# Shift and scale columns ahead of the first loop's blocks, and two gates computed early and parked in DRAM

## The chip, the cores and the metric

The kernel runs on one core of a Trainium2 chip. The metric is the device time of one execution in microseconds, the median of several runs. TensorE (PE in the rows) does matmuls and their weight loads (PEld), VectorE is DVE, ScalarE is ACT, GpSimd is POOL and SyncE is SP. Each engine runs its own instructions in the order of the program and waits where an input or a buffer isn't ready.

## The reference, cut to what matters

One block of a diffusion model on x (512 tokens of 1024 columns) with a context of 256 tokens:

```python
mx = split(silu(c) @ w_mod + b_mod, 6)         # shift, scale, gate, shift, scale, gate of x
mc = split(silu(c_ctx) @ w_mod + b_mod, 6)     # the context uses shift and scale only
hx = rms_norm(x, g_mix) * (1 + mx[1]) + mx[0]
hc = rms_norm(ctx, g_mix) * (1 + mc[1]) + mc[0]
conv, qa, kva, kr, gates = split(hx @ w_in)    # the context: hc @ w_in for kva and kr alone
y_conv = silu(layer_norm(depthwise(a * sigmoid(g)))) @ w_pw          # a, g = split(conv)
y_mla = attention(qa, kva, kr, kva_c, kr_c) @ w_o                    # 8 heads
x = x + mx[2] * ((sigmoid(g_conv) * y_conv + sigmoid(g_mla) * y_mla) @ w_out)   # split(gates)
x = x + mx[5] * swiglu(modulate(rms_norm(x), mx[3], mx[4]));  out = rms_norm(x)
```

## The kernel before

Everything lies transposed: 128 columns of the model on the partitions, tokens along the row, so x is eight tiles of 128x512. A float32 product is made of three matmuls: each operand is split into a high part (a cast on ScalarE, `wh`, `ph`) and a low part (the difference, on VectorE, `wl`, `pl`), and high by high, high by low and low by high are added. A projection of 128 columns, `gemm`, is thus 24 matmuls of 128x512. Weights come as tiles of 512 KB (`wr`), each split in two halves of 512 columns; six halves of high and of low parts are held at a time.

**Ahead of the loop** the squares of x are added up, column sums over the partitions (`colsum`, fp32, each matmul two records) give the rms, GpSimd takes the power, and a 128x512 matmul broadcasts it (`spread`). `warm` issues matmuls of ones that nothing reads.

**The first loop** goes over the eight 128-row blocks k of x. Block k needs its shift and scale, two 128-entry columns that are dot products of silu(c) with 1024 rows of w_mod. Before, a block's slabs (1 MB) are multiplied and added on VectorE (`gemv`, six of eight 128x256 slabs) and finished on TensorE (`mod_sum`: the two others and the sum over partitions, 12 records). Then t = x * rms * (1 + scale), hh is its high part plus shift on ScalarE and hl the low part on VectorE, and 18 matmuls add the block to six accumulators (the query and key-value latents and the rotary key). ScalarE scales the same slabs by silu(c_ctx) and GpSimd adds them up for the context (`ctx_steps`, `ctx_sum`).

**The section behind it** normalises the latents, computes the first two convolution inputs (`conv_steps`: two gemms of 24 matmuls, a tanh, a multiply-add and a split; `pump` issues so many of its steps between other work), the context's modulated hc, the context's key-value latent (`pkv`, 48 matmuls of 128x256 from two weights `wk`), and then the first query projection (`prep_qr`). `rc = bcast(dg_c, C)` broadcasts the context's rms from the diagonal `dg_c`. From the first load to the first head's values the order of all engines is the order of the code; behind that, a scheduler sets it when the program is built.

**The tail** of the attention computes sixteen gates (`gate`: a gemm and a tanh): eight for the attention, eight for the convolution. `tot` adds up the eight convolution outputs and `mean` is a matmul of ones with it.

The lines that the rows name: L126 and L122 are the low and high part of a weight, L262 the multiply-add of `gemv`, L272 `mod_sum`, L278 `warm`, L184 `spread`, L189 `colsum`, L583 t, L600, L604 and L606 the loop's matmuls, L318 the matmuls of a stepped gemm, L643 the latents' multiply-add, L728 and L734 the context's, L795 the additions of `tot`, L212 the multiply-adds of the later modulation vectors.

Of the kernel before, what the change touches and what calls it, by code (L numbers as in the profile page):

```python
# [62 lines left out]
def block_kernel(ctx: ExitStack, tc: tile.TileContext, I, out):  # L63
# [186 lines left out]
    def slab(k, kc):  # L250
        return mods[k][kc // 2][:, (kc % 2) * 256:(kc % 2) * 256 + 256]

    gm, sss = [], {}

    def gemv(k, a, b):
        if a == 0:
            gm.append(bp.tile([P, 512], F32, tag="ph", name=nm("gm"), bufs=3)[:, 0:256] if PE_KC[k] < 8 else None)
        for kc in range(a, min(b, 8 - PE_KC[k])):
            if kc == 0:
                dve.tensor_scalar(out=gm[k], in0=slab(k, kc), scalar1=sc[:, kc:kc + 1], scalar2=None, op0=ALU.mult)  # L260
            else:
                dve.scalar_tensor_tensor(out=gm[k], in0=slab(k, kc), scalar=sc[:, kc:kc + 1],  # L262
                                         in1=gm[k], op0=ALU.mult, op1=ALU.add)

    def mod_sum(k, m=None, n=0):
# [1 line left out]
        for j in range(2):
            ops = [(slab(k, kc), sc[:, kc:kc + 1]) for kc in range(8 - n, 8)]
            if m is not None:
                ops.append((m, ones[:, 0:1]))  # L270
            for i, (l, r) in enumerate(ops):
                pe.matmul(ps[:, j:j + 1], lhsT=l[:, j * P:(j + 1) * P], rhs=r, start=i == 0, stop=i == len(ops) - 1)  # L272
        return ps
# [17 lines left out]

    def ctx_steps():
        for k in range(KD):
            for kc in range(KD):
                act.activation(slab(k, kc), slab(k, kc), AF.Copy, scale=sc[:, 8 + kc:9 + kc])
                if kc == KD - 1:
                    ctx_sum(k)
                yield

    def ctx_sum(k):  # L300
        md = mods[k]
# [889 lines left out]
```

## Time and profile before

| | |
|---|---|
| median of 3 runs | 1043.89 us (1043.16 to 1043.91) |
| the profiled execution | 1043.18 us, span 1041.4 us |
| TensorE busy | 1007.6 us, 97% of the span |
| VectorE, ScalarE, GpSimd busy | 582.9, 459.1, 213.2 us |
| granted clock of TensorE, mean | 0.988 |
| read from HBM | 108.65 MB, 106 GB/s over the span |

The span is the time from the first to the last instruction of the profiled execution; its own time is 1.8 us longer. A granted clock of 1.00 is 2.4 GHz, 0.50 is 1.2 GHz. Where a row of the timeline ends with brackets, the engine was idle for so long before it, and the name is that of what ended the wait.

### The profile page before, as it was taken

How to read it: one execution, taken by the hardware profiler on the slowest of the kernel's cores; microseconds unless marked ns; L12 is line 12 of the kernel's file. 1: busy time of each engine (PE TensorE's matmuls, PEld its weight loads, DVE VectorE, ACT ScalarE, POOL GpSimd, SP SyncE). 2: the span in 40 equal slices, each digit the busy share in tenths (PEclk: the TensorE clock that was granted, in tenths of full speed). 3: DMA queues.
4: the chain of work that ended last, by engine and by line, in shares of the span. 5: the costliest groups of instructions: out<-in, count | busy, mean ns of one | idle time of the engine just before them, and what ended most of it. 6: DMA issues, size and time to landing. Idle time of an engine off the chain costs nothing.

```text
span 1041.4 us, 14089 instructions
## 1 busy us (share of the span) xinstructions
PE 1007.6 (97%) x5156; PEld 851.9 (82%) x5156; DVE 582.9 (56%) x1006; ACT 459.1 (44%) x864; POOL 213.2 (20%) x343
## 2 busy tenths in 40 slices
PE   8789999999999999999999999999999999999996
PEld 7567788888888888788878888988888888888886
DVE  6997774655654554436797774744643333433332
ACT  4567465555555555634382233442333333322322
POOL 2767503252352435420000000300000000000000
PEclk9889999999999999999999999999999999999998
DMA  9901543554554626752637754132633223233312
GB/s 329 332 13 48 125 141 95 134 137 114 161 127 110 155 53 161 202 148 87 213 118 249 225 169 140 61 112 101 212 101 100 82 102 100 89 86 106 92 56 81
DMA packets 52117, 137.11 MB, mean 132 GB/s; under 512 B 8784, under 2 KB 10960, under 8 KB 52048
## 3 DMA queue, kind: packets, MB, share of 16 engines
q1 hardware_dynamic: 41808, 110.77, 33.0%
q0 software_dynamic: 10240, 25.44, 10.4%
q8 instruction: 40, 0.66, 0.3%
q14 instruction: 29, 0.24, 0.1%
HBM read 108.65 MB, written 2.10 MB: 106 GB/s over the span
## 4 chain that ended last, share of the span: by engine, by line
PE 82%; DVE 7%; DMA 3%; issue 3%; ACT 2%; POOL 2%; SPq 0%; POOLq 0%; DVEq 0%; ACTq 0%
PE px L138 13%; PE px L139 13%; PE px L140 13%; PE ps L139 9%; PE ps L138 9%; PE ps L140 9%; PE px L318 6%; PE ps L475 3%; DVE gm L262 2%; PE ps L476 2%; PE px L495 2%; DMA ur<-u 1%; DMA p<-in_w_q_dram 1%; PE px L439 1%; POOL ur L338 1%
## 5 line engine op out<-in xcount | busy, mean ns | idle before, releaser
L126 DVE TENSOR_TENSOR wl<-wr,wh 128x512 fp32r<-128x512 f32 (+2 forms) x280 | 189.5, 683 | 251.9 <-ACT wh L122 245.0
L122 ACT CAST wh<-wr 128x512 fp32r<-128x512 f32 (+1 forms) x290 | 174.5, 610 | 317.8 <-PE ps L139 138.0
L139 PE MATMUL px<-a,wh 128*128 128x512 f32 (+1 forms) x607 | 223.9, 369 | 2.7 <-DVE a L734 2.1
L138 PE MATMUL px<-a,wh 128*128 128x512 f32 (+1 forms) x607 | 224.5, 371 | 0.9 <-ACT a L105 0.6
L140 PE MATMUL px<-a,wl 128*128 128x512 f32 (+1 forms) x607 | 223.4, 368 | 0.0
L139 PE MATMUL ps<-a,wh 128*128 128x512 f32 (+1 forms) x376 | 141.5, 376 | 0.8 <-DVE a L933 0.8
L138 PE MATMUL ps<-a,wh 128*128 128x512 f32 (+1 forms) x376 | 141.5, 376 | 0.0
L140 PE MATMUL ps<-a,wl 128*128 128x512 f32 (+1 forms) x376 | 141.2, 375 | 0.0
L139 PEld LDWEIGHTS px<-a,wh 128*128 128x128 f32 x607 | 114.9, 189 | 23.2 <-DVE a L734 2.5
L138 PEld LDWEIGHTS px<-a,wh 128*128 128x128 f32 x607 | 114.9, 189 | 21.4 <-ACT a L105 1.4
L140 PEld LDWEIGHTS px<-a,wl 128*128 128x128 f32 x607 | 115.1, 190 | 18.7
L174 POOL TENSOR_TENSOR s<-s,mhalf 128x2 f32<-128x2 f32 (+1 forms) x10 | 9.4, 937 | 585.2 <-DVE s L172 585.2
L338 POOL DMA_DIRECT2D ur<-u x128 | 67.9, 538 | 114.0 <-issue 58.2
L139 PEld LDWEIGHTS ps<-a,wh 128*128 128x128 f32 x376 | 70.7, 188 | 14.1 <-DVE a L933 1.5
L138 PEld LDWEIGHTS ps<-a,wh 128*128 128x128 f32 x376 | 70.8, 188 | 12.9
L140 PEld LDWEIGHTS ps<-a,wl 128*128 128x128 f32 x376 | 70.7, 188 | 12.8
L352 POOL DMA_DIRECT2D a<-e x128 | 63.1, 499 | 86.6 <-ACT e L350 69.5
L318 PE MATMUL px<-a,wh 128*128 128x512 f32 x256 | 80.7, 393 | 0.0
L475 PE MATMUL ps<-a,a 128*128 128x512 f32 x160 | 58.1, 399 | 0.0
L318 PEld LDWEIGHTS px<-a,wh 128*128 128x128 f32 x256 | 47.1, 188 | 9.5
L212 DVE SCALAR_TENSOR_TENSOR a<-p,sc,a 128x512 f32<-128x512 f32 x56 | 40.7, 747 | 20.9 <-DMA p<-in_w_mod_dram 20.5
L318 PE MATMUL px<-a,wl 128*128 128x512 f32 x128 | 50.2, 392 | 0.0
(202 smaller groups left out, 1550.3 us busy)
## 6 DMA issues: line engine op xcount, KB each, us to landing
wr<-in_w_dram SPq DMA_DIRECT2D x60, 512.0 KB, 3.4
wr<-in_w_in_dram SPq DMA_DIRECT2D x35, 512.0 KB, 3.7
ur<-u POOLq DMA_DIRECT2D x128, 130.0 KB, 4.3
p<-in_w_mod_dram SPq DMA_DIRECT2D x64, 256.0 KB, 4.2
a<-in_w_mod_dram SPq DMA_DIRECT2D x32, 256.0 KB, 5.7
a<-e POOLq DMA_DIRECT2D x128, 64.0 KB, 2.0
wr<-in_w_dwx_dram SPq DMA_DIRECT2D x8, 512.0 KB, 3.6
wr<-in_w_o_dram SPq DMA_DIRECT2D x8, 512.0 KB, 4.9
```

What stands on the lines that cost most here:

```text
L122: act.copy(h, raw[:, i * WB:i * WB + h.shape[-1]])
L126: (eng or dve).tensor_tensor(out=l, in0=raw[:, i * WB:i * WB + h.shape[-1]], in1=h.bitcast(F32), op=ALU.subtract)
L138: pe.matmul(ps, lhsT=wh, rhs=ah, start=first, stop=False)
L139: pe.matmul(ps, lhsT=wh, rhs=al, start=False, stop=False)
L140: pe.matmul(ps, lhsT=wl, rhs=ah, start=False, stop=last)
L212: dve.scalar_tensor_tensor(out=acc[e], in0=md, scalar=sc[:, kc:kc + 1], in1=acc[e], op0=ALU.mult, op1=ALU.add)
L262: dve.scalar_tensor_tensor(out=gm[k], in0=slab(k, kc), scalar=sc[:, kc:kc + 1], in1=gm[k], op0=ALU.mult, op1=ALU.add)
L318: pe.matmul(ps, lhsT=l, rhs=r, start=k == 0 and i == 0, stop=k == n - 1 and i == 2)
L338: pool.dma_start(out=ur[32 * s_:32 * s_ + 32].bitcast(F32), in_=u[32 * g:32 * g + 32, :, 8 * s_:8 * s_ + UW].bitcast(F32))
L352: pool.dma_start(out=parts[j][32 * g:32 * g + 32, :], in_=e[32 * j:32 * j + 32, j:j + S])
L475: pe.matmul(s[:, 0:512], lhsT=l[:, q0:q0 + P], rhs=rx_, start=i == 0, stop=i == 4)
L476: pe.matmul(s[:, 512:768], lhsT=l[:, q0:q0 + P], rhs=rc_, start=i == 0, stop=i == 4)
```

## The change

The shift columns of a block come from eight fp32 matmuls with two columns on the right (`shift_dots`, for c and c_ctx together), two blocks ahead. The scale column of a block comes from one VectorE instruction of 128x1024 (`scale_dot`, which multiplies transposed weights with a row `crow` of silu(c) on all partitions and accumulates along the row), one block ahead. `gemv`, `mod_sum`, `ctx_steps` and `ctx_sum` go, and with them GpSimd's additions; all low parts of the loop are VectorE's. The context's scale takes eight more such dots (`ctx_dots`) behind the loop, from the same weights loaded again. The nine warming matmuls stand right ahead of the loop, the last three go.

In the section behind, all of conv 0 is issued first, the column sums of the context's squares are 16 matmuls instead of GpSimd additions and two, conv 1 is issued whole ahead of hc, and the first two convolution gates are computed between the context's steps and written to DRAM. In the tail these two gates are loaded back.

```diff
-PE_KC = (2, 2, 2, 2, 2, 2, 2, 2)
+EARLY = 2
...
     def load_mod(k):
-        t = [slot() for _ in range(4)]
-        for j in range(4):
-            sp.dma_start(out=t[j], in_=I["w_mod01"][k, :, 2 * j:2 * j + 2, :])
-        mods.append(t)
+        t = [slot() for _ in range(2)]
+        for j in range(2):
+            sp.dma_start(out=t[j], in_=I["w_mod0"][k, :, 512 * j:512 * j + 512])
+        mods.append((t, load_md(k)))
...
+    def row_dot(md, row, col):
+        dve.scalar_tensor_tensor(out=md, in0=md, scalar=1.0, in1=row, op0=ALU.mult, op1=ALU.mult, accum_out=col)
...
+    def shift_dots(k):
         ps = tiny(2)
...
+        for kc in range(8):
+            pe.matmul(ps, lhsT=mods[k][0][kc // 4][:, (kc % 4) * P:(kc % 4 + 1) * P], rhs=sc[:, 2 * kc:2 * kc + 2],
+                      start=kc == 0, stop=kc == 7)
+        act.copy(mod_s[:, 2 * k:2 * k + 2], ps)
+
+    def scale_dot(k):
+        row_dot(mods[k][1], crow, mod_s[:, 16 + k:17 + k])
...
+    def gate_steps(i):
+        ps = ps_x()
+        yield from mm_steps(ps, gate_ws[i], hx)
+        t = slot()
+        act.activation(t, ps, AF.Tanh, scale=0.5)
+        pool.dma_start(out=spill[i], in_=t)
...
-        warm(WARM[1])
+        r = rstd_cols(st, D, 4)
+        scale_dot(0)
+        shift_dots(0)
         w = w_slots(768)
         w_hi(w, wq[0])
-        gemv(0, 0, GA)
-        r = rstd_cols(st, D, 4)
-        w_lo(w, wq[0], pool)
-        gemv(0, GA, 8)
-        ps = mod_sum(0, gm[0], PE_KC[0])
+        ss = shift_scale(0)
         bc = spread(r, 4, tiny)
-        warm(WARM[2])
+        shift_dots(1)
+        warm(WARM[1])
...
+            if nxt:
+                scale_dot(k + 1)
+            dve.scalar_tensor_tensor(out=hl, in0=t, scalar=ss[:, 0:1], in1=hh.bitcast(F32), op0=ALU.add, op1=ALU.subtract)
+            for j in range(6):
+                pe.matmul(accx[j], lhsT=wc(w[0], j * P), rhs=hh, start=k == 0, stop=False)
             if nxt:
                 w2 = w_slots(768)
                 w_hi(w2, wq[k + 1])
...
+                ss = shift_scale(k + 1)
+                w_lo(w2, wq[k + 1])
+            if k + 2 < KD:
+                shift_dots(k + 2)
...
+        def ctx_dots():
+            for k in range(KD):
+                row_dot(mds[k], ccrow, mod_s[:, 24 + k:25 + k])
+                if k + 4 < KD:
+                    mds.append(load_md(k + 4))
+                yield
...
+        pump(steps, 12)
+        bc_q = bcast(dg_q, S)
+        latent_lo(latent_t(accx[2:4], "g_kv", bc_kv, kva, S), kva)
         rope_sum(accx[4], tk, 0)
...
+        cw += [split_w(load_c[2])]
+        for i, sq in enumerate(cq):
+            colsum(st_c, sq, 2, i == 0, i == KD - 1)
+        pump(steps, 99)
+        raw8 += [load_w(I["w_in"][19 + i]) for i in range(EARLY)]
+        tq = latent_t([accx[0], accx[1], q2], "g_q", bc_q, qa, S)
+        r_c = rstd_cols(st_c, D, 2)
+        cw += [split_w(load_c[3])]
+        latent_lo(tq, qa)
+        dg_c = diag(r_c, C)
+        pump(dots, 4)
+        gate_ws[0] = split_w(raw8[0])
...
+        pump(dots, 99)
+        steps = conv_steps(1, cw[2], cw[3])
+        u1 = next(steps)
+        pump(steps, 12)
         rc = bcast(dg_c, C)
         pump(steps, 99)
...
+            if k == 0:
+                gate_ws[1] = split_w(raw8[1])
             if k in WK_AT:
-                wk.append(split_w(load_w8[len(wk)], D, pool if LO_P[1 + len(wk)] else dve))
-        pump(steps, CONV1)
+                pump(gates, 24)
+                wk.append(split_w(load_w8[len(wk)]))
+        pump(gates, 99)
...
-        sg_conv = [gate(19 + i, o_t[6]) for i in range(2)]
+        sg_conv = []
+        for i in range(EARLY):
+            t = slot()
+            act.copy(t[:, 0:1], o_t[6][:, 0:1])
+            sp.dma_start(out=t, in_=spill[i])
+            sg_conv.append(t)
```

On VectorE, in the first loop, one block before (`gm` is the running sum of the slabs `a`, `s` the block's shift and scale, `p` the weight):

```order
L260 TENSOR_SCALAR gm_575<-a_341,sc 128x256
L262 SCALAR_TENSOR_TENSOR gm_575<-a_341,sc,gm_575 128x256
L262 SCALAR_TENSOR_TENSOR gm_575<-a_342,sc,gm_575 128x256
L282 TENSOR_SCALAR s_579<-px_541,vec 128x1
L283 TENSOR_SCALAR s_579<-px_541,bm_86,vec 128x1
L583 SCALAR_TENSOR_TENSOR t_582<-a_120,s_579,a_276 128x512
L262 SCALAR_TENSOR_TENSOR gm_575<-a_342,sc,gm_575 128x256
L262 SCALAR_TENSOR_TENSOR gm_575<-a_343,sc,gm_575 128x256
L591 SCALAR_TENSOR_TENSOR a_99<-t_582,s_579,a_98 128x512
L262 SCALAR_TENSOR_TENSOR gm_575<-a_343,sc,gm_575 128x256
L126 TENSOR_TENSOR wl_587<-p_349,wh_585 128x512
L126 TENSOR_TENSOR wl_588<-p_349,wh_586 128x256
```

The same block's worth after (`md` is the transposed weight, `row` is crow):

```order
L563 SCALAR_TENSOR_TENSOR t_455<-a_123,s_413,a_280 128x512
L257 SCALAR_TENSOR_TENSOR md_285,mod_s<-md_285,row_133 128x1024
L570 SCALAR_TENSOR_TENSOR a_101<-t_455,s_413,a_100 128x512
L279 TENSOR_SCALAR s_472<-mod_s,bm_90,vec 128x1
L120 TENSOR_TENSOR wl_468<-p_287,wh_466 128x512
L120 TENSOR_TENSOR wl_469<-p_287,wh_467 128x256
```

Six instructions on `gm` and two small ones become one long dot and one small one, and the order between t, the low part of the activation (L591, now L570) and the weight's low parts stays.

On VectorE, in the section, before, from the variance of the context (L172) to hc (L626 is the diagonal dg_c, L650 the low parts of the query latent, L332 and L106 the end of conv 0):

```order
L172 TENSOR_SCALAR s_1002<-px_822 128x2
L712 TENSOR_TENSOR s_1006<-px_822,vec 128x8
L713 TENSOR_TENSOR s_1006<-px_822,bm_86 128x8
L714 TENSOR_TENSOR s_1006<-s_1006,vec 128x8
L626 TENSOR_TENSOR a_1010<-cst,s_1004 128x256
L650 TENSOR_TENSOR a_812<-a_989,a_811 128x512
L650 TENSOR_TENSOR a_814<-a_992,a_813 128x512
L650 TENSOR_TENSOR a_816<-a_995,a_815 128x512
L332 SCALAR_TENSOR_TENSOR t_954<-t_954,px_956 128x512
L106 TENSOR_TENSOR u_823<-t_954,u_823 128x512
L728 SCALAR_TENSOR_TENSOR t_1070<-a_351,s_1006,a_1035 128x256
L728 SCALAR_TENSOR_TENSOR t_1074<-a_351,s_1006,a_1035 128x256
```

After, from the end of conv 0 (L312, L100) to the diagonal (L617); `px_697` holds the column sums:

```order
L312 SCALAR_TENSOR_TENSOR t_792<-t_792,px_794 128x512
L100 TENSOR_TENSOR u_698<-t_792,u_698 128x512
L634 SCALAR_TENSOR_TENSOR a_870<-ps_110,vec,a_808 128x512
L634 SCALAR_TENSOR_TENSOR a_873<-ps_110,vec,a_808 128x512
L634 SCALAR_TENSOR_TENSOR a_876<-a_709,vec,a_808 128x512
L166 TENSOR_SCALAR s_879<-px_697 128x2
L120 TENSOR_TENSOR wl_885<-wr_679,wh_883 128x512
L120 TENSOR_TENSOR wl_886<-wr_679,wh_884 128x512
L641 TENSOR_TENSOR a_687<-a_870,a_686 128x512
L641 TENSOR_TENSOR a_689<-a_873,a_688 128x512
L641 TENSOR_TENSOR a_691<-a_876,a_690 128x512
L617 TENSOR_TENSOR a_894<-cst,s_881 128x256
```

The diagonal stood ahead of the three low parts and of conv 0's end; now it stands behind conv 0's end, three products of the latent, two low parts of conv 1's second weight and three low parts of the latent. On TensorE the matmul that reads it, the broadcast rc, stands behind the first 12 of conv 1's 48 matmuls.

On VectorE, in the tail, before (`a_4888` is tot):

```order
L126 TENSOR_TENSOR wl_5010<-wr_5005,wh_5008 128x512
L795 TENSOR_TENSOR a_4888<-a_1634,a_2116 128x512
L126 TENSOR_TENSOR wl_5011<-wr_5005,wh_5009 128x512
L795 TENSOR_TENSOR a_4888<-a_4888,a_2503 128x512
L795 TENSOR_TENSOR a_4888<-a_4888,a_2985 128x512
L795 TENSOR_TENSOR a_4888<-a_4888,a_3372 128x512
L126 TENSOR_TENSOR wl_5062<-wr_5057,wh_5060 128x512
L795 TENSOR_TENSOR a_4888<-a_4888,a_3854 128x512
L795 TENSOR_TENSOR a_4888<-a_4888,a_4201 128x512
L795 TENSOR_TENSOR a_4888<-a_4888,a_4541 128x512
L126 TENSOR_TENSOR wl_5063<-wr_5057,wh_5061 128x512
```

After (`a_4846` is tot, `px_4860` the mean):

```order
L120 TENSOR_TENSOR wl_4951<-wr_4945,wh_4949 128x512
L120 TENSOR_TENSOR wl_5000<-wr_4995,wh_4998 128x512
L782 TENSOR_TENSOR a_4846<-a_1592,a_2074 128x512
L120 TENSOR_TENSOR wl_5001<-wr_4995,wh_4999 128x512
L782 TENSOR_TENSOR a_4846<-a_4846,a_2461 128x512
L782 TENSOR_TENSOR a_4846<-a_4846,a_2943 128x512
L782 TENSOR_TENSOR a_4846<-a_4846,a_3330 128x512
L782 TENSOR_TENSOR a_4846<-a_4846,a_3812 128x512
L782 TENSOR_TENSOR a_4846<-a_4846,a_4159 128x512
L782 TENSOR_TENSOR a_4846<-a_4846,a_4499 128x512
L793 SCALAR_TENSOR_TENSOR a_1592<-px_4860,a_1592 128x512
```

Before, tot's additions stood between low parts of the weights; now one stands ahead of the low part wl_5001 and six stand behind it. On TensorE the mean's matmul stood behind seven gates in a row, the last two of them those that are moved; now it stands behind the five for the attention, and the weight of wl_5001 belongs to the third gate behind the mean.

## Rows read from the trace of the kernel before

**Rows 1.** The page, part 1: busy us, share of the span, instructions.

```profile
PE 1007.6 (97%) x5156; PEld 851.9 (82%) x5156; DVE 582.9 (56%) x1006; ACT 459.1 (44%) x864; POOL 213.2 (20%) x343
```

**Rows 2.** Busy time by stage: us, each engine's busy us, granted clock, DMA.

```profile
21.30:82.60 61.30, 51.03 (x229) 41.19 (x230) 59.00 (x79) 39.03 (x91) 44.42 (x35) 0.89 0.49 179
82.60:126.90 44.30, 40.22 (x212) 33.22 (x211) 32.76 (x54) 24.32 (x51) 24.72 (x29) 0.96 0.34 93
```

**Rows 3.** Groups by line and shape, VectorE, 21 to 83 us.

```profile
L262 DVE SCALAR_TENSOR_TENSOR gm<-a,sc,gm 128x256 f32<-128x256 f32 x32 | 27.8, 867 | 0.7
L583 DVE SCALAR_TENSOR_TENSOR t<-a,s,a 128x512 f32<-128x512 f32 x7 | 8.8, 1254 | 0.3
```

**Rows 4.** Timeline of VectorE, section: start, us, operation, count.

```profile
97.52 1.40 DVE L643 SCALAR_TENSOR_TENSOR a<-ps,vec,a 128x512 f32<-128x512 f32 x2
...
118.28 0.48 DVE L728 SCALAR_TENSOR_TENSOR t<-a,s,a 128x256 f32<-128x256 f32 x1
118.68 0.48 DVE L734 SCALAR_TENSOR_TENSOR a<-t,s,a 128x256 fp32r<-128x256 f32 x1
```

**Rows 5.** The page, part 5: multiply-adds of later modulation vectors.

```profile
L212 DVE SCALAR_TENSOR_TENSOR a<-p,sc,a 128x512 f32<-128x512 f32 x56 | 40.7, 747 | 20.9 <-DMA p<-in_w_mod_dram 20.5
```

**Rows 6.** Timeline of TensorE, first loop, two stretches.

```profile
58.83 0.50 PE L272 MATMUL px<-sc,a 128*128 128x1 f32 x4
...
60.09 1.19 PE L604 MATMUL ps<-a,wl 128*128 128x512 f32 x4
...
78.36 1.20 PE L600 MATMUL ps<-a,wh 128*128 128x512 f32 x4 [0.52 <-ACT a L584]
...
82.59 0.62 PE L318 MATMUL px<-a,wh 128*128 128x512 f32 x2
```

**Rows 7.** Short stretches: busy us and granted clock around idle TensorE.

```profile
45.00:47.10 2.10, 0.00 (x1) 0.01 (x1) 2.10 (x2) 0.78 (x2) 1.80 (x2) 1.00 0.98 293
47.30:57.40 10.10, 10.10 (x31) 8.35 (x31) 9.96 (x16) 6.54 (x17) 5.15 (x4) 0.50 0.32 128
57.40:63.00 5.60, 5.60 (x31) 4.58 (x29) 5.49 (x9) 1.99 (x6) 4.69 (x4) 0.98 0.00 0
116.50:118.40 1.90, 0.03 (x1) 0.00 (x0) 1.90 (x5) 0.61 (x2) 1.60 (x4) 1.00 1.04 323
119.00:122.50 3.50, 3.33 (x15) 3.21 (x15) 2.72 (x6) 2.38 (x5) 0.00 (x0) 0.51 1.05 214
```

**Rows 8.** Timeline of TensorE ahead of the first loop.

```profile
8.83 2.62 PE L278 MATMUL px<-ones 128*128 128x128 f32 x22
12.95 1.05 PE L189 MATMUL px<-ones,a 128*128 128x1 f32 x8 [1.50 <-DVE a L544]
13.87 2.25 PE L278 MATMUL px<-ones 128*128 128x128 f32 x18
...
18.05 1.10 PE L184 MATMUL px<-t,ones 128*128 128x512 f32 x2 [0.69 <-DVE t L179]
18.98 0.83 PE L278 MATMUL px<-ones 128*128 128x128 f32 x6
21.33 0.96 PE L600 MATMUL ps<-a,wh 128*128 128x512 f32 x3 [1.52 <-ACT a L584]
```

**Rows 9.** Timeline of ScalarE, tail.

```profile
472.84 0.62 ACT L122 CAST wh<-wr 128x512 fp32r<-128x512 f32 x1 [1.15 <-PE px L139]
...
478.28 0.62 ACT L122 CAST wh<-wr 128x512 fp32r<-128x512 f32 x1 [1.14 <-PE px L139]
```

**Rows 10.** Timeline of ScalarE, section.

```profile
90.58 1.14 ACT L122 CAST wh<-wr 128x512 fp32r<-128x512 f32 x2
```

**Rows 11.** Timeline of VectorE, tail.

```profile
473.49 0.69 DVE L126 TENSOR_TENSOR wl<-wr,wh 128x512 fp32r<-128x512 f32 x1 [2.03 <-ACT wh L122]
474.10 0.69 DVE L795 TENSOR_TENSOR a<-a,a 128x512 f32<-128x512 f32 x1
...
479.54 2.14 DVE L795 TENSOR_TENSOR a<-a,a 128x512 f32<-128x512 f32 x3
```

More of the change, by code (lines that the diff above doesn't have):

```diff
@@ L73, in block_kernel @@
     pp = ctx.enter_context(tc.tile_pool(name="pp", bufs=1, space=PSUM))
+    dp = ctx.enter_context(tc.tile_pool(name="dp", bufs=1, space=bass.MemoryType.DRAM))
+    spill = [dp.tile([P, S], F32, name=f"spill{i}") for i in range(EARLY)]
+    gate_ws = [None] * EARLY
     count = [0]
@@ L248, in block_kernel @@
     tiny = ps_x
[L250 to L265, printed above, removed]
-        ps = tiny(2)
[L267 to L273, printed above, removed]
+    def row_dot(md, row, col):
+        dve.scalar_tensor_tensor(out=md, in0=md, scalar=1.0, in1=row, op0=ALU.mult, op1=ALU.mult, accum_out=col)
+    mod_s = cp.tile([P, 32], F32, name="mod_s")
+    def shift_dots(k):
+        ps = tiny(2)
+        for kc in range(8):
[4 more added lines that the diff above has]
+        row_dot(mods[k][1], crow, mod_s[:, 16 + k:17 + k])
     def warm(n):
@@ L290, in pump @@
                 break
[L292 to L301, printed above, removed]
-        for i, j in ((0, 1), (2, 3), (0, 2)):
-            pool.tensor_tensor(out=md[i], in0=md[i], in1=md[j], op=ALU.add)
-        if k % 2 == 0:
-            mcs.append(slot())
-        pool.tensor_tensor(out=mcs[-1][:, k % 2 * 256:k % 2 * 256 + 256], in0=md[0][:, 0:256], in1=md[0][:, 256:512], op=ALU.add)
     kva, qa, kvac, cw = [], [], [], []
@@ L533, in block_kernel @@
             xs.append(t)
-        load_mod(0)
+        crow = row_tile(0)
         sp.dma_start(out=ident, in_=I["cst"][:, 0:128])
-        load_mod(1)
-        load_mod(2)
-        load_mod(3)
+        for k in range(4):
+            load_mod(k)
         ssq = slot()
@@ L563, in block_kernel @@
                 load_mod(k + 4)
-            if k == 1:
+            if k == 3:
+                ccrow = row_tile(1)
+                sp.dma_start(out=cst[:, 128:1152], in_=I["cst"][:, 128:1152])
+                load_c = [load_w(I["w_in"][3 + o]) for o in (KD, 0)]
+            if k == 4:
+                mats = slot()
+                sp.dma_start(out=mats, in_=I["cst"][:, 1152:1664])
                 cs = [slot() for _ in range(4)]
@@ L608, in block_kernel @@
                 w = w2
+        mds = [load_md(k) for k in range(4)]
+        load_c.append(load_w(I["w_in"][3 + 1]))
+        act.activation(ccrow, ccrow, AF.Silu)
+        def ctx_dots():
[4 more added lines that the diff above has]
+                yield
+        dots = ctx_dots()
         def squares(srcs, n):
@@ L659, in block_kernel @@
             kvac.append((h_[:, 0:C], h_[:, C:2 * C]))
-        def ctx_mods(a, b):
-            for k in range(a, b):
-                m = mcs[k // 2][:, k % 2 * 256:k % 2 * 256 + 256]
-                for j in range(2):
-                    pe.matmul(pm[:, j * 8 + k:j * 8 + k + 1], lhsT=m[:, j * P:(j + 1) * P], rhs=ones[:, 0:1], start=True, stop=True)
         misc = tiny()
-        st_kv, st_q, st_c, st_c2, pm = misc[:, 0:4], misc[:, 4:8], misc[:, 8:10], misc[:, 10:12], misc[:, 16:32]
+        st_kv, st_q, st_c, st_c2 = misc[:, 0:4], misc[:, 4:8], misc[:, 8:10], misc[:, 10:12]
+        raw8 = []
         steps = conv_steps(0, cw[0], cw[1])
         u0 = next(steps)
-        pump(steps, 5)
         kq = squares(accx[2:4], S)
@@ L682, in block_kernel @@
         act.copy(stackr, mats)
-        cw += [w_slots(D)]
-        w_hi(cw[2], load_c[2])
-        cq = squares(ctxs[:CQ], C)
-        pump(steps, 6)
-        colsum(st_q, qs_, 4, True, True)
-        r_q = rstd_cols(st_q, 384, 4)
-        pump(steps, 6)
+        pump(steps, 5)
         bc_kv = bcast(dg_kv, S)
-        cq += squares(ctxs[CQ:], C)
-        for sq in cq[1:]:
-            pool.tensor_tensor(out=cq[0], in0=cq[0], in1=sq, op=ALU.add)
         dg_q = diag(r_q, S)
+        cq = squares(ctxs, C)
+        pump(steps, 12)
+        bc_q = bcast(dg_q, S)
+        latent_lo(latent_t(accx[2:4], "g_kv", bc_kv, kva, S), kva)
         rope_sum(accx[4], tk, 0)
```

106 lines of the change are left out of this document (38 added, 68 removed).

## The prediction

> **What bounds the kernel now.** The page's first part is read first: TensorE is busy 97% of the span [rows 1], so only stretches in which it isn't can give much, and work taken from it or put on it counts in full. The busy time by stage shows where it isn't: in the first loop it is busy 51.03 of 61.30 us while VectorE is busy 59.00, and in the section behind it 40.22 of 44.30 [rows 2]. In the loop VectorE is the bound, and it is slow there: a multiply-add of 128x256 takes 0.87 us on average and one of 128x512 1.25 [rows 3], where the same kinds take 0.48 [rows 4] and 0.75 [rows 5] elsewhere; GpSimd is busy 44.42 us of the same stretch [rows 2]. TensorE's chain says the same: 18 wide matmuls alone take 4.23 us (78.36 to 82.59), 12 narrow records 1.26 (58.83 to 60.09) [rows 6], and a whole block with both 5.60 [rows 7], but eight blocks took 61.3. The clock rows come last: it fell to 0.50 (1.2 GHz instead of 2.4) behind stretches of about 2 us in which TensorE did nothing (45.00:47.10, 116.50:118.40), and one fall lasted 10.1 us of a busy TensorE, with narrow matmuls inside [rows 7].
>
> **The loop.** Five or six 128x256 operations a block leave VectorE, and one of 128x1024 comes. Its price isn't in the trace. From 0.48 for 256 columns [rows 4] and 0.747 for 512 [rows 5] each further 256 cost 0.27, so 1024 cost 1.28 without whatever accumulating adds; the upper bound is the ratio of 1254 to 747 ns that this kind showed under disturbance [rows 3, 5], 2.15. VectorE's block is then 0.7 + 1.3 + 0.7 + 0.2 + about 1.0 for the weights' low parts, 3.9 or at most 4.8 us. TensorE's is 5.60 less 1.26 plus 16 narrow records (8 fp32 matmuls of two columns, two records each, at 0.105) 1.68: 6.0, for six blocks, and 4.23 for the last two, which sum no more shifts: 44.5 us. So TensorE becomes the bound whichever price the dot has. ScalarE loses eight scalings a block, GpSimd everything, the loads fall to about 1.4 MB a block; no transfer at all ran in 57.40:63.00 [rows 7], so I cost transfers at nothing; that cover goes if loads arrive slower than a block in 6 us.
>
> The loop starts later. Column sums run from 12.95 to 13.87 as before [rows 8]; 8 records took 0.92, so each set of 16 for the shifts 1.84. The first set ends at 15.7; the broadcast, at 18.05 before behind VectorE, comes some 0.9 earlier since VectorE has one dot ahead of it and not eight operations (0 to 0.9), takes 0.93 to 18.1; the second set ends at 19.9; the nine warming matmuls, which took 2.1, at 22.0, against 21.33. Loop end: 22.0 + 44.5 = 66.5, against 82.59: 16.1 less.
>
> From that I take the clock. Before, the nine warming matmuls stood right behind the column sums; now from 11.45 (the end of the first 34 [rows 8]) to 19.9 TensorE has one wide broadcast and otherwise narrow columns or nothing. The nearest row is 47.30:57.40: at half clock one block took 10.1 us instead of 5.6, a loss of 4.5 [rows 7], and nine warming matmuls at half rate may lose up to 1.0. The smallest is 1.7, half of the 3.5 us of 119.00:122.50 [rows 7]; nothing, if it doesn't fall. I take 5.0: **11.1 less.**
>
> **The section behind it**, T counted from the loop's end. TensorE first: conv 0 is 48 matmuls, at 5.44 us for 24 [rows 9] 10.9; two broadcasts and the rope sum 2.8; 16 column-sum records 1.8 and 32 for the context's squares 3.4; a wait for a PSUM buffer and one for the tanh behind eight squares, some 1.0 (0 to 2): T = 19.9. Twelve matmuls of conv 1 then end at 22.6, and the next instruction is the broadcast of the context's rms, rc. Its input, dg_c, ends a chain on VectorE which starts when conv 0 ends, by the order shown above: multiply-add 0.7, cast on ScalarE 0.57 [rows 10], low part 0.69 [rows 11], to 21.9; three latent products 0.7 each [rows 4] to 24.0; two weight low parts, which wait for five casts on ScalarE, to 26.6; three low parts 2.0 to 28.6; the diagonal 0.4 to 29.0. TensorE waits **6.4 us** with two thirds of conv 1 queued behind. GpSimd's power, by its own row under 1 us, is hidden in it.
>
> VectorE then has four dots 5.1, the first gate's low parts 1.35, four dots 5.1: 40.6. Conv 1 ends on TensorE at 38.2, so its tail of 2.0 on VectorE follows at once: 42.6; three tiny ones 0.3; sixteen context operations at 0.40 apart [rows 4] 6.4; three weight splits 4.0; some 1.7 of waiting on ScalarE between them (0 to 3): 55.0. TensorE had the two gates, 10.9, by 49.1, then waits for hc's last low part, has 27 matmuls of 128x256 left, 3.1, and the column-sum chain of about 2.3 that conv 1 no longer covers: the query projection starts at 60.4, against 44.3 before [rows 2]: **16.1 more**, of which the two gates are 10.9. A half clock behind the 6.4 us idle mostly falls into the wait for hc; 0.5 for it (0 to 3). 16.6 together.
>
> The dots are the price that matters here, eight of them in VectorE's chain. The row nearest to a dot, a multiply-add with two fp32 sources in SBUF and no accumulator output, goes through at full rate, 747 ns for 512 [rows 5]. The Trainium skill says otherwise for the dot: its page "Vector Engine (DVE) Microarchitecture Reference", section "7. Points that are easy to get wrong", states that this kind of instruction with two sources in SBUF that aren't bf16 halves its throughput, since no read port is left for the accumulator. The row contradicts it for the form without the output, and no run here shows the form with it; by the rule the section would be some 7 to 8 us longer, by the row nothing.
>
> **The tail.** Two gates leave: 10.9 less. But they also stood between the last mla gate and the mean of the convolution. By the order above the six remaining additions of tot now stand behind the low part wl_5001. Before, the low part of the first half behind the mean (473.49 [rows 11], by the order above) came 0.65 us after a ScalarE cast (472.84 [rows 9]) that waited for TensorE's release of a weight half. Six halves are held, so this was the sixth half before it, and the mean came five halves of 2.72 later, at 486.4. wl_5001 is of the sixth half behind the mean, so the half that frees its buffer is the last one ahead of the mean. Low part 0.6 us after TensorE is through, itself 0.6, six dependent additions at 0.72 (2.14 for 3 [rows 11]) 4.3: the mean waits **5.5 us**. Before, the last addition ended at 481.7 [rows 11], 4.7 ahead of the mean, so there it cost nothing. Half clock behind an idle stretch of that length: 1.7 [rows 7] (0 to 4). The reloads from DRAM and the two one-column copies hide behind five gates. Tail: **3.7 less.**
>
> **Sum.** -11.1 + 16.6 - 3.7 = +1.8, against the profiled execution's own 1043.18 (span 1041.4 and 1.8 around it): 1045.0. The median of the runs is 1043.89, 0.7 higher, so 1045.0 to 1045.7; I forecast 1045.0. A change under 0.2% (2.1 us) can't be told from none here.
>
> **Rivals.**
> 1. *The clock doesn't fall at the loop's start* (or for 1.7 only). For it: before, TensorE idled 1.5 us ahead of 12.95 and waited again up to 21.33 [rows 8] without a fall. Against it: there the nine wide matmuls lay in the middle. 1040.0.
> 2. *The section's chain is shorter*: ScalarE casts early, VectorE without GpSimd beside it, and no extra waiting: the stall at rc 4 us instead of 6.4 and hc's end 3 us earlier, so 5 less: 1040.0.
> 3. *The accumulating dot takes 2.15 us*, the disturbed rate, because it must also write its sum. In the loop that's covered (4.8 of 6.0); in the section all eight stand in VectorE's chain, with hc's last low part behind them: 8 x 0.87 = 7 more, 1052.0, slower. It decides from about 1.3 + 0.2 us a dot on, where the sum passes 0.2%.
>
> **How the numbers follow.** The forecast has 0.42 (own range 1042 to 1048), rival 1 0.20, rival 2 0.16, rival 3 0.22. Faster by over 0.2% (below 1041.8): most of rivals 1 and 2 and a tenth of the forecast, 0.32. Slower (above 1046): rival 3 and four tenths of the forecast, 0.39; the rest, 0.29, between. Low: rivals 1 and 2 with their ends, 1035.5; both together (1035) are left out. High: rival 3 with a costlier clock, 1055.
>
> **What would show it.** Loop: 16 narrow records a block, blocks 6.0 apart at full clock, VectorE half idle, granted clock 0.5 somewhere between 13 and 35. Section: one TensorE wait of about 6 us on rc's broadcast released by VectorE, a second of some 3 us in the context projection, query projection about 60 behind the loop's end. Tail: six additions back to back behind a low part, and TensorE waiting about 5 us for the mean. The prediction is wrong if the dot is dear, if the clock stays up or stays down for several blocks, or if the section's DMA comes late, since a late weight would lengthen the same chain.

## The result, and the profile after

The changed kernel runs in 1050.24 us, median of 12 runs (1044.45 to 1051.18), against 1043.03 for the kernel before (12 runs, 1041.28 to 1044.86). The ratio is 1.0059, 95% interval 1.0045 to 1.0073: **slower by 0.6%**. The forecast was 1045.0, its own range 1042 to 1048, the range with the rivals 1035.5 to 1055.0. The profiled execution was the fastest of the twelve, 1044.45 us with a span of 1042.7, so 1.3 us of span more than before; the mean granted clock in it was 0.985, over the twelve 0.9808.

From the page of the changed kernel, the span and part 1:

```profile
span 1042.7 us, 14009 instructions
...
PE 1008.4 (97%) x5178; PEld 854.9 (82%) x5178; DVE 554.7 (53%) x994; ACT 438.3 (42%) x818; POOL 150.6 (14%) x294
```

TensorE's busy time is what it was [rows 1]; VectorE has 28 us less, GpSimd 63. TensorE's timeline, in the start and the loop, at the loop's end (69.84) and at the first query projection (132.44):

```profile
12.47 1.05 PE L183 MATMUL px<-ones,a 128*128 128x1 f32 x8 [1.46 <-DVE a L530]
13.39 1.93 PE L264 MATMUL px<-sc,a 128*128 128x2 f32 x16
17.05 2.07 PE L178 MATMUL px<-t,ones 128*128 128x512 f32 x2 [1.74 <-DVE t L173]
18.92 3.41 PE L264 MATMUL px<-sc,a 128*128 128x2 f32 x16
22.19 4.06 PE L274 MATMUL px<-ones 128*128 128x128 f32 x18
26.00 1.17 PE L572 MATMUL ps<-a,wh 128*128 128x512 f32 x4
...
27.48 1.84 PE L264 MATMUL px<-sc,a 128*128 128x2 f32 x16
29.18 1.19 PE L583 MATMUL ps<-a,wl 128*128 128x512 f32 x4
...
33.41 1.84 PE L264 MATMUL px<-sc,a 128*128 128x2 f32 x16
...
69.84 0.62 PE L298 MATMUL px<-a,wh 128*128 128x512 f32 x2
...
132.44 0.48 PE L132 MATMUL px<-a,wh 128*128 128x512 f32 x1
```

The loop ends 12.75 us earlier than before [rows 6]. The section from there to the query projection takes 62.6 us, 18.3 more than before (44.3 [rows 2]), and what stands behind it is 4.2 shorter: together the 1.3 us more of span.

Blocks are 5.93 apart (27.48 to 33.41). But the loop starts at 26.00 instead of 21.33 [rows 8]: the second set of shift dots (18.92) took 3.41 and the nine warming matmuls 4.06, where the first set took 1.93 and the nine took 2.25 before. The granted clock, in the same execution, in four stretches:

```profile
15.50:26.50 11.00, 9.45 (x38) 8.37 (x39) 7.54 (x15) 3.41 (x10) 0.00 (x0) 0.53 1.04 401
87.00:92.00 5.00, 5.00 (x16) 3.96 (x16) 0.25 (x1) 0.00 (x0) 0.00 (x0) 0.66 0.36 108
97.00:106.00 9.00, 5.51 (x16) 4.39 (x17) 9.00 (x16) 2.00 (x5) 0.00 (x0) 0.62 0.38 116
...
486.50:491.00 4.50, 3.88 (x9) 2.47 (x10) 2.27 (x4) 1.07 (x2) 0.00 (x0) 0.62 0.12 49
```

Each row has the stretch, its length, the busy us of TensorE, its weight loads, VectorE, ScalarE and GpSimd, and last the granted clock, the DMA's share and GB/s. The clock is 0.53 before the loop starts, 0.66 at conv 0's end, behind the column sums of the context's squares, and 0.62 behind two waits. These are the waits of TensorE, by what ended them (total, times, longest):

```profile
PE px L625 <- DVE a L617: 6.0, 1, 6.0
PE px L790 <- DVE a L782: 5.5, 1, 5.5
PE px L133 <- DVE a L718: 2.1, 2, 1.9
```

L625 is the broadcast rc, L790 the mean, L133 the context projection, waiting for hc's low parts (L718): the three forecast waits. Section and tail on VectorE, and the mean on TensorE:

```profile
91.75 0.69 DVE L312 SCALAR_TENSOR_TENSOR t<-t,px 128x512 f32<-128x512 f32 x1 [4.83 <-PE px L298]
...
97.00 1.29 DVE L120 TENSOR_TENSOR wl<-wr,wh 128x512 fp32r<-128x512 f32 x2 [1.14 <-ACT wh L116]
98.21 1.89 DVE L641 TENSOR_TENSOR a<-a,a 128x512 fp32r<-128x512 f32 x3
100.02 0.42 DVE L617 TENSOR_TENSOR a<-cst,s 128x256 f32<-128x256 f32 x1
100.36 1.22 DVE L257 SCALAR_TENSOR_TENSOR md<-md,row 128x1024 f32<-128x1024 f32 x1
101.50 0.08 DVE L257 DVE_READ_ACCUMULATOR md<-md,row 128x1 f32 x1
101.50 1.22 DVE L257 SCALAR_TENSOR_TENSOR md<-md,row 128x1024 f32<-128x1024 f32 x1
...
126.85 0.48 DVE L718 SCALAR_TENSOR_TENSOR a<-t,ssc,a 128x256 fp32r<-128x256 f32 x1 [0.18 <-ACT a L715]
...
482.05 0.69 DVE L120 TENSOR_TENSOR wl<-wr,wh 128x512 fp32r<-128x512 f32 x1 [1.42 <-ACT wh L116]
482.66 4.32 DVE L782 TENSOR_TENSOR a<-a,a 128x512 f32<-128x512 f32 x6
```

```profile
487.12 2.05 PE L790 MATMUL px<-a,ones 128*128 128x512 f32 x2 [5.54 <-DVE a L782]
```

The diagonal (L617, 100.02) stands behind all that the prediction listed. A dot takes 1.22 us, its accumulator read 0.08, and the next starts 1.14 us after the first one's start. VectorE's chain from conv 0's end (L312, 91.75) to hc's last low part (126.85 and 0.48) is 35.6 us long. In the tail the six additions run back to back from 482.66 and end at 486.98; the mean follows at 487.12 after 5.54 idle.

### The profile page after: what moved, and what is told of

Same layout as the page of the kernel before. It is cut to its first block, busy times and chain, and to the rows that moved or that the text cites. A ratio compares the mean times of both kernels' runs of the same rounds, so it can differ in the third digit from the quotient of the medians.

```text
span 1042.7 us, 14009 instructions
## 1 busy us (share of the span) xinstructions
PE 1008.4 (97%) x5178; PEld 854.9 (82%) x5178; DVE 554.7 (53%) x994; ACT 438.3 (42%) x818; POOL 150.6 (14%) x294
## 4 chain that ended last, share of the span: by engine, by line
PE 88%; DVE 3%; DMA 3%; issue 2%; ACT 2%; POOL 1%; SPq 0%; POOLq 0%; DVEq 0%; ACTq 0%
PE px L132 13%; PE px L133 12%; PE px L134 12%; PE ps L133 9%; PE ps L132 9%; PE ps L134 9%; PE px L298 8%; PE ps L455 3%; PE px L475 2%; PE ps L456 1%; PE px L264 1%; DMA ur<-u 1%; DMA a<-e 1%; PE px L419 1%; PE px L183 1%
## 5 line engine op out<-in xcount | busy, mean ns | idle before, releaser
L116 ACT CAST wh<-wr 128x512 fp32r<-128x512 f32 (+2 forms) x290 | 174.4, 610 | 312.2 <-PE ps L133 144.5
L132 PE MATMUL px<-a,wh 128*128 128x512 f32 (+1 forms) x591 | 218.6, 371 | 0.6 <-ACT a L99 0.6
L133 PE MATMUL px<-a,wh 128*128 128x512 f32 (+1 forms) x591 | 217.0, 368 | 2.1 <-DVE a L718 2.1
L134 PE MATMUL px<-a,wl 128*128 128x512 f32 (+1 forms) x591 | 216.8, 367 | 0.0
L133 PE MATMUL ps<-a,wh 128*128 128x512 f32 (+1 forms) x376 | 141.6, 377 | 0.8 <-DVE a L925 0.8
L133 PEld LDWEIGHTS px<-a,wh 128*128 128x128 f32 x591 | 111.5, 189 | 22.3 <-DVE a L718 2.7
L134 PEld LDWEIGHTS px<-a,wl 128*128 128x128 f32 x591 | 111.5, 189 | 18.2
L298 PE MATMUL px<-a,wh 128*128 128x512 f32 x288 | 91.9, 401 | 0.4 <-ACT a L627 0.4
L133 PEld LDWEIGHTS ps<-a,wh 128*128 128x128 f32 x376 | 70.7, 188 | 14.3 <-DVE a L925 1.5
L134 PEld LDWEIGHTS ps<-a,wl 128*128 128x128 f32 x376 | 70.8, 188 | 12.8
L332 POOL DMA_DIRECT2D a<-e x128 | 63.0, 498 | 90.8 <-ACT e L330 69.8
L298 PEld LDWEIGHTS px<-a,wh 128*128 128x128 f32 x288 | 54.6, 193 | 12.6 <-ACT a L627 1.1
L298 PE MATMUL px<-a,wl 128*128 128x512 f32 x144 | 57.7, 401 | 0.0
```

Of the source, the lines that this page charges most:

```text
L116: act.copy(h, raw[:, i * WB:i * WB + h.shape[-1]])
L132: pe.matmul(ps, lhsT=wh, rhs=ah, start=first, stop=False)
L133: pe.matmul(ps, lhsT=wh, rhs=al, start=False, stop=False)
L134: pe.matmul(ps, lhsT=wl, rhs=ah, start=False, stop=last)
L298: pe.matmul(ps, lhsT=l, rhs=r, start=k == 0 and i == 0, stop=k == n - 1 and i == 2)
L332: pool.dma_start(out=parts[j][32 * g:32 * g + 32, :], in_=e[32 * j:32 * j + 32, j:j + S])
```

## The experiments

The kernels ran in three groups, each on one chip together with the kernel before, and each ratio is to that: the changed kernel again and e1 to e3 (the kernel before: 1044.41 us), e5 to e8 (1043.76), e9 to e12 (1044.35). Across groups the ratios are the fairer comparison. There are 12 runs of each, but 10 of e7 and 6 of e6, e8, e10, e11 and e12.

| kernel | median us | ratio, interval | mean clock | clock loss | rest |
|---|---|---|---|---|---|
| changed, again | 1049.32 | 1.0051 [1.0032, 1.0070] | 0.9807 | 20.3 | 1029.4 |
| e1 warming behind column sums | 1047.36 | 1.0032 [1.0010, 1.0053] | 0.9823 | 18.5 | 1028.7 |
| e2 two gates ahead of the mean | 1042.05 | 0.9975 [0.9960, 0.9991] | 0.9842 | 16.4 | 1025.6 |
| e3 rms early | 1046.86 | 1.0025 [1.0011, 1.0039] | 0.9831 | 17.7 | 1029.1 |
| e5 rms and four dots early | 1043.12 | 0.9997 [0.9984, 1.0011] | 0.9842 | 16.4 | 1027.1 |
| e6 gates back in the tail | 1048.02 | 1.0050 [1.0032, 1.0068] | 0.9810 | 19.9 | 1028.8 |
| e7 three times nine warming | 1048.77 | 1.0046 [1.0027, 1.0065] | 0.9842 | 16.5 | 1031.8 |
| e8 combination | 1036.13 | 0.9916 [0.9893, 0.9940] | 0.9892 | 11.2 | 1024.0 |
| e9 start without idling | 1048.93 | 1.0041 [1.0019, 1.0062] | 0.9821 | 18.8 | 1030.3 |
| e10 e8 with e9's start | 1036.17 | 0.9913 [0.9892, 0.9934] | 0.9877 | 12.8 | 1023.4 |
| e11 e8 with all dots early | 1032.91 | 0.9880 [0.9855, 0.9906] | 0.9880 | 12.4 | 1020.4 |
| e12 e11 with e9's start | 1032.11 | 0.9878 [0.9854, 0.9902] | 0.9888 | 11.5 | 1021.0 |

"Clock loss" is the mean over a kernel's runs of (1 - granted clock) x span, "rest" the mean of time less that. It is an estimate, since half clock costs nothing where TensorE waits anyway. It sorts the runs of the changed kernels: the changed kernel's times scatter by 2.0 us (standard deviation of 12), its rest by 0.8; e1's by 3.65 and 0.65. It doesn't sort those of the kernel before: 35 runs in the first group scatter by 2.2 us, and their rest by 2.2 too (mean clock 0.9838, loss 16.9, rest 1027.7). So these two columns are hints.

**The changed kernel, again.**

> The changed kernel unchanged, profiled again beside the others. Its profiled execution ran in 1044.45 us at a mean granted clock of 0.985, most others in about 1050 at 0.980. Theory A (the extra time is more half clock at the loop's start): 1050, the clock rows at 0.50 reach some 10 us further than 26 us. Theory B (the clock falls again behind the 6.0 us wait on rc's broadcast or the 5.5 us wait on the mean, for longer): the loop starts at 26 as before and the extra 0.50 stands behind 96 or behind 487.

The loop started at 26.2 again, and the profile (1048.04 us) has half clock where the first had none. The same stretches as above, of this execution:

```profile
15.50:26.50 11.00, 9.44 (x39) 8.32 (x39) 7.54 (x15) 3.56 (x10) 0.00 (x0) 0.56 1.04 401
...
128.50:133.00 4.50, 4.46 (x25) 4.39 (x25) 1.34 (x3) 1.05 (x3) 1.64 (x3) 0.62 0.73 228
486.50:491.00 4.50, 1.18 (x3) 0.69 (x3) 3.04 (x5) 0.00 (x0) 0.00 (x0) 0.64 0.72 227
491.00:495.00 4.00, 4.00 (x11) 2.77 (x10) 3.09 (x6) 2.37 (x4) 0.00 (x0) 0.55 0.00 0
```

128.5 to 133, behind the wait for hc, is at 0.62 here and was at 1.00 in the first profile. The mean starts at 489.82 here, and half clock lasts 4.8 us from there, against 3.2 from 487.12 in the first. The span is 3.5 us longer: 0.55 of it lies ahead of the loop's end (70.39 for 69.84), 2.15 between there and the query projection, 0.8 behind the mean's start. That is theory B for this execution, though the fall that it shows in the section stands behind the wait for hc and not behind rc. It ran in 1048.04, and none of the runs at 1050 and more of the changed kernel was profiled.

**e1.**

```diff
         scale_dot(0)
+        warm(WARM[1])
         shift_dots(0)
...
         shift_dots(1)
-        warm(WARM[1])
+        warm(WARM[2])
```

> The nine warming matmuls back behind the column sums, where they stood, the last three back ahead of the loop. Theory A (the clock fell because TensorE had only narrow columns, one broadcast and idling from 11.5 to 19): full clock at the loop's start, loop from about 21 instead of 26, 5 us less than the changed kernel in a profile like the first, and up to 10 less where the extra half clock of most runs lies here too. Rival (nine short matmuls don't hold it): loop from 26 or later, same time as the changed kernel.

Its profiled execution had full clock to 83 us, the loop from 21.19 and 1040.24 us, 7.8 less than the changed kernel's in the same group. But the other eleven runs reach to 1053.0, at clocks down to 0.978, and the median is only 2.0 lower. One profile agrees with theory A, the median doesn't.

**e7.** On e1: nine more ahead of the second set, and nine instead of three ahead of the loop:

```diff
         bc = spread(r, 4, tiny)
+        warm(WARM[1])
         shift_dots(1)
-        warm(WARM[2])
+        warm(WARM[1])
```

> Nine warming matmuls behind the column sums, nine behind the broadcast and nine right ahead of the loop. With nine behind the column sums alone the profile showed full clock at the start, but the runs spread from 1040 to 1053. Theory A (in the slower ones the clock still fell at the loop's start): the loop starts at about 23, the spread shrinks, the median is 1043 to 1045, the mean granted clock 0.985 or more. Rival (the slower ones lose it elsewhere, in the section and the tail, by chance): median 1047 to 1048 and the same spread.

It failed: 1048.77, and in the profile the clock fell anyway while the first nine ran. Timeline of TensorE in e7:

```profile
12.91 1.05 PE L183 MATMUL px<-ones,a 128*128 128x1 f32 x8 [2.34 <-DVE a L530]
13.83 3.31 PE L274 MATMUL px<-ones 128*128 128x128 f32 x18
16.93 3.41 PE L264 MATMUL px<-sc,a 128*128 128x2 f32 x16
20.20 2.05 PE L178 MATMUL px<-t,ones 128*128 128x512 f32 x2
```

2.34 us idle stood ahead of the column sums, nine warming matmuls took 3.31 instead of 2.25, the dots 3.41.

**e9.**

```diff
-WARM = (34, 9, 3)
+WARM = (44, 9, 4)
...
         scale_dot(0)
+        warm(WARM[1])
         shift_dots(0)
...
         bc = spread(r, 4, tiny)
+        warm(WARM[2])
         shift_dots(1)
-        warm(WARM[1])
```

> The changed kernel with ten more warming matmuls ahead of the column sums, so that TensorE doesn't idle there for 1.5 to 2.4 us, nine behind them, four behind the broadcast, and none right ahead of the loop. In three profiles of four with nine matmuls behind the column sums or ahead of the loop the clock had fallen by 14 to 16 us, at once behind that idle stretch. If that idling is what lets it fall: full clock at the start in the profile, loop from 21 to 22, median 1043 to 1045, spread below 2 us. Rival (narrow columns let it fall whatever stands before): half clock from 16 to 20 on, 1048 to 1050.

The idle stretch is gone, and the clock held longer, and fell all the same:

```profile
13.22 0.95 PE L183 MATMUL px<-ones,a 128*128 128x1 f32 x8
14.04 2.25 PE L274 MATMUL px<-ones 128*128 128x128 f32 x18
16.13 1.84 PE L264 MATMUL px<-sc,a 128*128 128x2 f32 x16
...
19.67 1.84 PE L264 MATMUL px<-sc,a 128*128 128x2 f32 x16
22.39 1.70 PE L573 MATMUL ps<-a,wh 128*128 128x512 f32 x4 [0.88 <-ACT a L565]
...
24.75 3.40 PE L264 MATMUL px<-sc,a 128*128 128x2 f32 x16
```

The first dots took 1.84, full rate; the first block's matmuls run at half (the dots inside it 3.40) after the second dots and 0.88 of idling. The clock rows of this execution are at 0.50 from 23 to 33. So idling ahead of the column sums is not the whole cause, and the first case fell; the rival's time came true (1048.93), its place, 16 to 20, didn't. Nor does the code alone decide: e1 and e8 (below) are the same up to the second set of dots, and TensorE idled 1.93 and 1.87 us ahead of the column sums; e1 kept full clock, in e8 it fell between 14 and 15, and in e11, with e8's start, between 19 and 20. What holds the clock at the start stays open: a start without 32 narrow records ahead of the loop wasn't tried.

**e2.**

```diff
+        sg_conv += [gate(19 + i, o_t[6]) for i in (2, 3)]
         mean = ps_x()
         pe.matmul(mean, lhsT=ones, rhs=tot, start=True, stop=True)
...
-        for i in range(2, 7):
+        for i in range(4, 7):
```

> Two convolution gates issued ahead of the mean's matmul, as before, but not the two that are parked. If the 5.5 us wait for the mean comes from the six additions of tot behind a low part whose buffer the last gate ahead of the mean frees: the wait goes, 5.5 us less and 1.5 to 2 more for the half clock behind it, 7 less than the changed kernel, no wait on tot in the rows. Rival (the wait moves to the layer norm's chain or to the next gates' weights): under 2 us less.

1042.05, 7.3 less than the changed kernel: the wait is gone, its half clock too, as forecast. In e2 the last additions of tot (VectorE) end at 491.75, behind another low part, and the mean (TensorE) comes 4.8 us later:

```profile
489.61 2.14 DVE L782 TENSOR_TENSOR a<-a,a 128x512 f32<-128x512 f32 x3
```

```profile
496.54 1.02 PE L791 MATMUL px<-a,ones 128*128 128x512 f32 x2
```

**e3.**

```diff
         for i, sq in enumerate(cq):
             colsum(st_c, sq, 2, i == 0, i == KD - 1)
+        r_c = rstd_cols(st_c, D, 2)
+        dg_c = diag(r_c, C)
         pump(steps, 99)
...
-        r_c = rstd_cols(st_c, D, 2)
         cw += [split_w(load_c[3])]
         latent_lo(tq, qa)
-        dg_c = diag(r_c, C)
```

> The context's rms and its diagonal made right behind the column sums, ahead of conv 0's end on VectorE. Theory V (the section is bound by VectorE's chain from 91.8 to 127.3, and the wait on rc only took time that TensorE would wait for hc's low parts later): the 6.0 us wait goes, the wait in the context projection grows by as much, the query projection starts at most 1 us earlier, time as the changed kernel, within 2 us (some of the half clock may come back). Rival T (the wait on rc is on TensorE's path): 6 us less, up to 9 with the clock.

2.5 us less, and the wait moved. TensorE's waits in e3, the rows of TensorE that had them, and the two ends of VectorE's chain:

```profile
PE px L298 <- ACT wh L116: 5.1, 1, 5.1
...
PE px L298 <- DVE wl L120: 1.8, 1, 1.8
```

```profile
105.26 0.50 PE L298 MATMUL px<-a,wl 128*128 128x512 f32 x1 [1.83 <-DVE wl L120]
...
115.64 1.22 PE L298 MATMUL px<-a,wh 128*128 128x512 f32 x2 [5.10 <-ACT wh L116]
```

```profile
91.67 0.69 DVE L312 SCALAR_TENSOR_TENSOR t<-t,px 128x512 f32<-128x512 f32 x1 [1.70 <-PE px L298]
...
127.08 0.48 DVE L718 SCALAR_TENSOR_TENSOR a<-t,ssc,a 128x256 fp32r<-128x256 f32 x1 [0.18 <-ACT a L715]
```

rc no longer waits and conv 1 runs through, but the two early gates, whose matmuls have the same line L298, now wait: the first for its weight's low part (1.8), the second for its weight's high part (5.1), whose cast stands on ScalarE behind the first of the context's, and that waited 1.63 us for VectorE. VectorE's chain is as long as it was, 35.9 us for 35.6. The query projection starts 61.4 us behind the loop's end instead of 62.6 in the first profile of the changed kernel and 64.8 in the second; counted the same way, conv 0 ended 1.6 earlier than in the first, without half clock there. That is theory V, with both of its bounds, 1 us and 2 us, just passed. By the table's estimate the 2.5 us are clock (17.7 for 20.3) and not rest (1029.1 for 1029.4).

**e5.** On e3, and the dots:

```diff
         r_c = rstd_cols(st_c, D, 2)
+        pump(dots, 1)
         dg_c = diag(r_c, C)
+        pump(dots, 3)
...
-        pump(dots, 4)
```

> As the run with the context's rms made early, and the first four context dots also moved ahead of conv 0's end, into 4.8 us in which VectorE idled. Theory V (the section is bound by VectorE's chain to hc, whatever TensorE waits for on the way): the query projection starts 4 to 6 us earlier than in the changed kernel, counted from the loop's end (57 to 59 instead of 62.6), and the median is 1043 to 1046. Rival T (the dots are hidden and only the wait on rc counts): as the run with the rms alone, 1047.

1043.12, and the query projection 59.3 behind the loop's end, just past 57 to 59: theory V. VectorE's chain is 30.0 us long here:

```profile
93.95 0.68 DVE L312 SCALAR_TENSOR_TENSOR t<-t,px 128x512 f32<-128x512 f32 x1
...
123.47 0.49 DVE L719 SCALAR_TENSOR_TENSOR a<-t,ssc,a 128x256 fp32r<-128x256 f32 x1 [0.18 <-ACT a L716]
```

The four dots in VectorE's gap bring 3.7 us more than e3 by the medians and 2.9 by the ratios, about as much as taking away the wait beside it (2.5, by the ratios 2.7).

**e6.**

```diff
-EARLY = 2
+EARLY = 0
...
-        gate_ws[0] = split_w(raw8[0])
...
-            if k == 0:
-                gate_ws[1] = split_w(raw8[1])
...
+        sg_conv = [gate(19 + i, o_t[6]) for i in range(2)]
         mean = ps_x()
```

> The two early gates and their spill left out of the section and computed in the tail again, as before; all else as changed. Theory V (in the section they fill time that TensorE waits in anyway, so that only their weights' low parts, 2.6 us of VectorE, count): section 3 less, tail 10.9 more less the 5.5 us wait and its 1.8 of half clock, together the same as the changed kernel within 2 (1049 to 1052). Rival (they cost their 10.9 us of matmuls in the section): 1041 to 1043.

1048.02 against 1049.32, ratios 1.0050 and 1.0051, and the query projection 61.8 behind the loop's end with 10.9 us of matmuls less. TensorE's longest waits in e6:

```profile
PE px L132 <- ACT wh L116: 6.1, 1, 6.1
PE px L625 <- DVE a L617: 6.1, 1, 6.1
```

It waits 6.1 us more, for the context projection's weight. So the early gates cost the section almost nothing, and e2 against e6 shows their worth: 6.0 us by the medians (1048.02 to 1042.05), 7.8 by the ratios, once the mean doesn't wait for them.

**e8.** e5 and e2 together, with nine warming matmuls added behind the column sums.

> Warming matmuls behind the column sums and ahead of the loop, the context's rms and four dots early, two other gates ahead of the mean. If the three losses add up (start 4 to 5, section 4 to 6, tail 7): 1033 to 1036, below both kernels. If they share the same half clock, 1037 to 1040.

1036.13: the upper figure of the first case, though not for its reason. Its profile had half clock from 14 to 29, so the start gave nothing there; section and tail add up: from 1049.32, e5's 6.2 and e2's 7.3 make 1035.8, and by the ratios 0.9921 for the measured 0.9916.

**e10.** e8 with e9's start.

> The same start on the combination that ran in 1036.1 (rms and four dots early, two gates ahead of the mean), whose profile had half clock from 14 to 29 and the loop from 28.2. If the start holds: 1029 to 1031. If not: 1035 to 1037.

1036.17. It didn't hold: half clock from 23 to 33.

**e11.** e8 with the dots in three gaps:

```diff
         act.copy(q2, accx[5])
+        pump(dots, 2)
         kq = added(kq)
...
         dg_q = diag(r_q, S)
+        pump(dots, 3)
...
-        pump(dots, 3)
+        pump(dots, 99)
```

> The combination with all eight context dots ahead of conv 0's end, in three gaps of VectorE (two behind the loop, three behind the diagonals, three behind the rms). If VectorE's chain from conv 0's end to hc still bounds the section: another 4 to 5 less, query projection 54 to 55 behind the loop's end, 1031 to 1032. Rival (TensorE's own matmuls, 47 us of them with two gates, are the bound by then, or ScalarE's casts): 0 to 2 less.

1032.91, 3.2 less, between the two. Timelines in e11, of TensorE the loop's end and the query projection, of VectorE conv 1's end:

```profile
69.73 0.61 PE L298 MATMUL px<-a,wh 128*128 128x512 f32 x2
...
125.36 0.48 PE L132 MATMUL px<-a,wh 128*128 128x512 f32 x1
```

```profile
103.15 0.69 DVE L312 SCALAR_TENSOR_TENSOR t<-t,px 128x512 f32<-128x512 f32 x1 [1.89 <-PE px L298]
```

55.6 us between loop's end and query projection, against 62.6 in the changed kernel. VectorE's chain is 27.4 us long (91.69 to 119.13), 2.6 less than in e8 though four dots left it: it now waits 1.89 us for conv 1 on TensorE, so the rival is right in part.

**e12.** e11 with e9's start.

> Both: the start without idling and all dots early. If both hold: 1025 to 1027, 17 below the kernel before. If the dots bring nothing: as the combination with the start alone.

1032.11, ratio 0.9878 [0.9854, 0.9902]: the fastest, 1.2% below the kernel before and 1.7% below the changed one, but not told apart from e11. Its profile had half clock at the start from 22 to 26 only.

## Why the prediction came out as it did

The terms held in the profiled execution; the step from it to the median, the clock's size, didn't.

- **Loop.** Block 6.0 forecast, 5.93 measured; the dot 1.28 forecast, 1.22 and 0.08 to read the accumulator, 1.14 from one to the next. The start with its half clock was put at 5.0 lost in the first block; it came earlier, in the second dots and the warming matmuls, and the loop started 4.0 later than 22.0 for it. Loop end 69.84 against 66.5 + 5.0 = 71.5: 12.75 gained instead of 11.1.
- **Section.** The wait on rc 6.0 for 6.4, broadcast at T = 30.7 for 29.0 (conv 0 ended 2.0 later, with half clock from 87 to 91 that I hadn't foreseen), hc's end T = 57.5 for 55.0, query projection 62.6 for 60.4. 18.3 more than before instead of 16.6. That VectorE's chain is the bound, not TensorE's wait, is shown by e3, which took the wait away and left the chain at 35.9 us for 35.6, and by e5 and e11, which shortened it to 30.0 and 27.4 and brought the query projection forward.
- **Tail.** The mean waited 5.54 for 5.5, in the place and behind the low part named; what stands behind the query projection got 4.2 shorter for 3.7. e2 takes 7.3 back, wait and clock.
- **Sum.** 1.8 forecast, 1.3 measured on the spans of the two profiled executions; this close because the loop's and the section's errors, 1.7 each, cancel. The median, 1050.24, lies outside the forecast's own 1042 to 1048, and inside the whole range only by rival 3, whose costly dot didn't happen: that part is luck. What failed is the step from one execution to the median: I sized each fall of the clock by one row and once. The mean granted clock of the twelve runs is 0.0042 below that of the profiled one, by the table's estimate 4.4 us of 1042.7. The second profile shows where 3.5 us can go: 2.15 in the section, with half clock from 129.0 to 132.8 behind the wait on hc, 0.8 more behind the mean. As an estimate, half of the time spent at half clock was lost, 1.9 of 3.8 us and 2.4 of 4.8; my terms for those two were 0.5 and 1.7, with ends of 3 and 4. Where the runs at 1050 lose the rest stays open. A lower clock alone need not cost it: the kernel before had 0.988 in its profile and a mean of 0.984 to 0.985 beside the experiments, with medians only 0.6 to 1.2 us above that profile's time.
- **Rivals.** Rival 3's time came out nearest, but not its mechanism: the dot takes 1.22 us, not 2.15. The page "Vector Engine (DVE) Microarchitecture Reference" of the Trainium skill, section "7. Points that are easy to get wrong", states half throughput for this kind of instruction with two sources in SBUF that aren't bf16. The sixteen dots of the trace average 1220 ns for 1024 elements, where the form without accumulator took 747 for 512 [rows 5], so here the measurement decides against it. (The 7 to 8 us that the prediction gives for this rule were too few: eight dots at twice its 1.28 us would have been 10.2 longer, as an estimate.) Rival 1 didn't happen: in the six profiles with the changed kernel's start (its own two, e2, e3, e5, e6) the clock fell between 14 and 17 us and rose between 25 and 29. Of the seven with another start e1's alone kept full clock, and e12's lost only 1.7 us, half clock from 22 to 25.4. Rival 2 didn't happen: the stall at rc was 6.0, and hc's end came later than forecast, not earlier.

## What to carry to other kernels

Work moved into an idle engine's time is only worth what isn't queued behind a later chain: here two gates came out almost free in the section and gave 6 us or more, but only when something else stood between the last weight split and the sum that waited for it. Look for the engine whose chain ends last, and fill its gaps, before removing another engine's wait beside it: taking away the 6.0 us wait on rc brought 2.5 us and left the chain as long as it was, eight dots moved into VectorE's gaps brought about 7. And cost each idle stretch of some microseconds on TensorE with its clock, over several executions: one profile may show the mildest.
